# State-space steps of two groups issued as one, with every operation of the stage in a fixed order

## The chip, the cores and the metric

The kernel runs on one core of a Trainium2 chip. The metric is the device time of one execution in microseconds (us). Engine names are those of the profile: PE is TensorE (matmuls; PEld are its weight loads), DVE is VectorE, ACT is ScalarE, POOL is GpSimd, and SP is the queue that issues loads.

## What is computed

One layer of a hybrid block on x of 1024 tokens x 1024 features, in float32. A first projection makes the inputs of two branches: a chunked gMLP (giving `y_a`) and a Mamba-2 state-space mixer (giving `y_b`). The change is in the second branch, which works on 32 heads of width 64 in 8 groups, on 8 chunks of 128 tokens:

```python
y_diag = jnp.einsum('bcgls,bcgrls,bcsgrp->bclgrp', cb, decay, xd)       # inside a chunk
chunk_states = jnp.einsum('bcsgn,bcgrs,bcsgrp->bcgrpn', bc, decay_to_end, xd)
# scan over the chunks: state * chunk_decay + chunk_states, giving prev_states
y_off = jnp.einsum('bclgn,bcgrpn,bcgrl->bclgrp', cc, prev_states, jnp.exp(a_cs))
y_b = y_diag + y_off + xh * d_skip[:, None]
yz = y_b * jax.nn.silu(ssm_z)                   # by groups of 256 features
y_b = rms_norm(yz, ssm_norm_w)                  # one mean square per token and group
merged = sigmoid(g_a) * (y_a @ w_proj_a) + sigmoid(g_b) * (y_b @ w_proj_b)
out = rms_norm(x + gate * (merged @ w_out), final_norm_w)
```

## The kernel before

**Stages.** Normalisation and the projections, the convolution and the gMLP mixing fill the execution up to about 908 us; then comes the stage that the change rewrites, the state-space steps, to about 1114 us; then the product with `w_proj_b` (units p1 to p7, whose first matmul writes the tile `x0p`) and the product with `w_out`. Products are in float32 that is split into a high and a low part, with three matmuls for one.

**A step.** One step is one group g (4 heads) on two chunks; s = 0 to 3 counts the steps of a group, and 32 steps make the stage. `order` (L1295) puts the groups in four rounds of two: (0,0), (1,0), (0,1), (1,1), and so on, so neighbours in `order` are the same s of two groups. Every step has these parts:

- *fetch*: two loads on SP's queue, `dcy` (cumulated decays, broadcast to 128 partitions) and `sl` (x, B, C and the gate of the two chunks).
- *mask* and *decay*: ACT makes `ea` by two exps (L1119), POOL masks `dcy` (L1123), ACT makes `dcy` by eight exps (L1131).
- *prep*: 12 rows of PE fill the banks `pc` (products of C and B, and B transposed) and `px` (x transposed); DVE multiplies `dcy` by `pc` (L1147) and makes `xd` and `xe` from `px` (L1150); ACT copies `bn` from `pc` (L1154).
- *front*: eight PE matmuls 128*64 into `yi` (inside the chunk), then `sp` (state increments; two matmuls 128*128, one where s = 3). DVE adds `sp` to the state that POOL multiplied by the chunk's decay (L1192, L1198 and L1200: chunk 0, then chunk 1, which needs chunk 0's), and adds the skip term to `yi` (L1180, two operations).
- *back*: PE multiplies the two states by C into `yn` (L1211; its second half needs the state after chunk 0), DVE scales it (`ym`, L1226), POOL adds it to `y` (L1228) and multiplies by the gate into `yz` (L1229).

**After every second step of a group** the mean squares follow: `yz` is stored, ACT squares it in place (L1251), POOL sums two tiles (L1255), four PE matmuls 128*32 (`pq`, here *strips*) sum over partitions, DVE makes a row (L1267), the row goes to memory and is read back as a column `ssq`, POOL takes the root by `pow` (L1282), and the root is stored. For the last two groups these are called *late* and fall behind the steps. They write where `yz` is, so they wait for its store.

**Beside the steps** PE works off the product `y_a @ w_proj_a` (`proj_a`, L1463): 8 column blocks of 24 draws, each draw two matmuls 128x512 into the banks `pma`, 384 in all. `draw(n)` puts n draws at its place in PE's order. For a block, ACT makes the high parts `wah` (L1377) and DVE the low parts `wal` (L1382, here *wal*); a gate by DVE closes the block (`tha`, L1488). The operands `yh` (ACT) and `yl` (DVE, L1360) come from `ya_operand(k)`, k = 0 to 7.

**What sets the order.** Each engine runs its instructions in order. `link(key, f)` puts an operation behind the last one linked on that engine; what isn't linked is put in by the scheduler, by its priority. `later(n, f)` runs f n slots of `run_tasks` later, and `beside_step` takes one waiting piece of work (a sum, a root). `load` issues on SP's queue in program order, and `store` on ACT's. Before, a step is: front of step n, decays of n+3, a piece of work, masks of n+4, 8 or 10 `pma`, back of n, prep of n+2.

## Time and profile before

| what | value |
|---|---|
| three runs | 1368.3 us median, 1366.72 to 1368.78 |
| the profiled execution | 1367.94 us, of which the profile's span is 1366.0 |
| clock granted to PE over the span | 0.999 |
| busy: PE, DVE, ACT, POOL | 1352.3, 1045.9, 799.2, 192.5 us |

The profile is one execution. A row of the timeline gives the start, the time to the end of the group and the instruction's form; consecutive instructions of one form stand in one row with their count. Starts are measured, ends of matmuls are modelled, and on every engine records overlap a little; so what an instruction costs its engine is read here from one start to the next. A row of a group gives the count, the busy time, the mean in ns, the idle time ahead of it and what ended that.

### The profile page before, as it was taken

To read this page: it belongs to the slowest core of one execution; us is meant where nothing else is said; L and a number is where in the kernel's file an instruction comes from. 1 tells how busy PE (TensorE), PEld (TensorE's weight loads), DVE (VectorE), ACT (ScalarE), POOL (GpSimd) and SP (SyncE) were. 2 spreads that over 40 slices of the span, in tenths; PEclk is the share of its full clock that TensorE was granted. 3 is DMA by queue.
4 is the path that set the end of the run, shared out by engine and by line. 5 is a ranking of instruction groups with operands and counts; after the bars stand their busy time and mean duration, and the time that the engine had idled before them with its cause. 6 is when DMAs were issued, how large, how long until landed. Compare 5 with 4: busy or idle time off the path is not lost.

```text
span 1366.0 us, 20176 instructions
## 1 busy us (share of the span) xinstructions
PE 1352.3 (99%) x6943; PEld 1116.6 (82%) x6943; DVE 1045.9 (77%) x1716; ACT 799.2 (59%) x1447; POOL 192.5 (14%) x191
## 2 busy tenths in 40 slices
PE   8999999999999999999999999999999999999997
PEld 7688888888888888888888888888888887888886
DVE  4786876777778888697887797458888866859976
ACT  5763666666666656466566556486877834233443
POOL 1000000000000000000000000006798971000002
PEclk9999999999999999999999999999999999999999
DMA  9674444334344657877656675589889959988903
GB/s 286 181 244 135 142 124 120 104 117 124 108 139 139 181 181 230 252 230 241 211 180 189 219 247 167 166 282 314 305 299 307 309 201 320 325 268 322 382 37 124
DMA packets 249530, 288.65 MB, mean 211 GB/s; under 512 B 16812, under 2 KB 196436, under 8 KB 249428
## 3 DMA queue, kind: packets, MB, share of 16 engines
q1 hardware_dynamic: 174868, 203.80, 46.9%
q10 hardware_dynamic: 74560, 83.57, 17.9%
q8 instruction: 55, 0.90, 0.3%
q14 instruction: 47, 0.39, 0.1%
HBM read 199.82 MB, written 87.49 MB: 210 GB/s over the span
## 4 chain that ended last, share of the span: by engine, by line
PE 92%; DMA 3%; DVE 2%; ACT 1%; SPq 1%; issue 0%; POOL 0%; POOLq 0%; DVEq 0%; ACTq 0%
PE xz L565 6%; PE xcb L565 6%; PE xx L565 6%; PE pma L82 6%; PE xuz L565 6%; PE xg L565 6%; PE ox L1867 3%; PE ycb L565 3%; PE vx L954 3%; PE yp L1676 3%; PE yz L565 3%; PE yx L565 3%; PE yg L565 3%; PE yuz L565 3%; PE yi L82 2%; PE sp L82 2%
## 5 line engine op out<-in xcount | busy, mean ns | idle before, releaser
L1123 POOL TENSOR_SCALAR_AFFINE_SELECT dcy<-dcy 128x1024 f32<-128x1024 f32 x32 | 35.3, 1103 | 790.6 <-ACT ea L1119 786.9
L1131 ACT ACTIVATE dcy<-dcy,nacs 128x128 f32<-128x128 f32 x256 | 78.3, 389 | 2.7 <-POOL dcy L1123 2.1
L1147 DVE TENSOR_TENSOR dcy<-dcy,pc 128x1024 f32<-128x1024 f32 x32 | 39.0, 1218 | 8.0 <-PE pc L85 6.4
L1229 POOL TENSOR_TENSOR yz<-y,sl 128x512 f32<-128x512 f32 x32 | 44.4, 1387 | 2.5
L82 PE MATMUL pma<-yh,wah 128*128 128x512 f32 x128 | 43.1, 418 | 0.0
L82 PE MATMUL pma<-yh,wal 128*128 128x512 f32 x128 | 42.5, 413 | 0.0
L82 PE MATMUL pma<-yl,wah 128*128 128x512 f32 x128 | 40.2, 396 | 0.0
L1119 ACT ACTIVATE ea<-dcy 64x512 f32<-64x512 f32 x64 | 39.8, 622 | 0.7 <-DMA dcy<-acs_d 0.3
L1024 ACT ACTIVATE ac<-ac 128x1024 f32<-128x1024 f32 x32 | 33.9, 1061 | 10.2 <-DVE ac L1022 10.0
L1614 DVE SCALAR_TENSOR_TENSOR yn<-yn,par,rb 128x512 f32<-128x512 f32 x32 | 25.4, 793 | 18.6 <-DMA yn<-yb_d 16.9
L1154 ACT COPY bn<-pc 128x256 f32<-128x256 f32 x32 | 11.9, 371 | 46.9 <-DVE dcy L1147 46.9
L1228 POOL TENSOR_TENSOR y<-y,ym 128x512 f32<-128x512 f32 (+1 forms) x32 | 37.0, 1155 | 1.9 <-DVE ym L1226 1.9
L1022 DVE SCALAR_TENSOR_TENSOR ac<-c2x,cwt,ac 128x1023 f32<-128x1023 f32 (+2 forms) x24 | 30.7, 1279 | 6.1 <-ACT ac L1020 6.0
L82 PE MATMUL yi<-dcy,xd 128*64 128x128 f32 x512 | 35.0, 279 | 0.0
L1022 DVE SCALAR_TENSOR_TENSOR ac<-c2cb,cwt,ac 128x1023 f32<-128x1023 f32 (+2 forms) x24 | 30.6, 1274 | 5.6 <-ACT ac L1020 5.5
L1882 POOL TENSOR_TENSOR r<-r,fnw 128x512 f32<-128x512 f32 x4 | 5.3, 1344 | 204.8 <-ACT junk L1880 204.8
L986 ACT ACTIVATE vm<-vm,vr 128x128 f32<-128x128 f32 x64 | 25.8, 484 | 14.2 <-DMA vm<-v_d 13.7
L1226 DVE TENSOR_TENSOR ym<-yn,ea 128x512 f32<-128x512 f32 (+1 forms) x32 | 19.9, 622 | 18.5 <-PE yn L82 18.4
L824 ACT CAST wbb<-wbr 128x512 fp32r<-128x512 f32 x32 | 19.8, 619 | 22.8 <-DMA wb_d<-wbb 17.0
L82 PE MATMUL sp<-xe,bn 128*128 128x256 f32 x112 | 32.7, 409 | 0.0
L82 PEld LDWEIGHTS yn<-sl,st 128*128 128x128 f32 x224 | 29.7, 191 | 2.8 <-POOL st L1192 0.4
L82 PEld LDWEIGHTS yi<-dcy,xd 128*64 128x64 f32 x512 | 27.3, 136 | 5.7 <-issue 3.1
(2963 smaller groups left out, 4372.8 us busy)
## 6 DMA issues: line engine op xcount, KB each, us to landing
sl<-s_d SPq DMA_DIRECT2D x32, 768.0 KB, 6.4
s_d<-ac ACTq DMA_DIRECT2D x32, 512.0 KB, 3.3
wb_d<-wbb ACTq DMA_DIRECT2D x32, 512.0 KB, 3.4
dcy<-acs_d SPq DMA_DIRECT2D x32, 512.0 KB, 5.3
av<-in_w_in_dram SPq DMA_DIRECT2D x36, 256.0 KB, 2.9
aw<-in_ada_w_dram SPq DMA_DIRECT2D x16, 512.0 KB, 6.6
...
```

What stands on the lines that cost most here:

```text
L82: pin(PE.matmul(acc, l, r, start=first, stop=last))
L565: pin(PE.matmul(ps, lw[:, k * P : (k + 1) * P], r[k], start=first and n + k == 0, stop=n == 2 and k == 3, skip_group_check=not first))
L954: pin(PE.matmul(ps[pn][j], l[:, j * P : (j + 1) * P], r, start=nm in ("p1", "p5", "p2") and n + units[i][1] == 0, stop=n == 2 and k == 3, ...
L1022: V.scalar_tensor_tensor(ac[:, s:], cc[:, : S - s], conv_wt[:, 3 - s, i : i + 1], ac[:, s:], op0=ALU.mult, op1=ALU.add)
L1119: link("A", lambda: A.activation(ea[hh * HD : (hh + 1) * HD], dcy.rearrange("p (j e) i l -> p e j (i l)", e=2)[hh * HD : (hh + 1) * HD, hh ...
L1123: link("G", lambda: G.affine_select(out=d8, in_=d8, compare_op=ALU.is_ge, fill=-1e30, base=0, pattern=[[0, 2 * HPG], [1, P]], channel_mult ...
L1131: link("A", lambda: A.activation(dcy[:, h, i, :], dcy[:, h, i, :], AF.Exp, bias=sub[:, i, h : h + 1]))
L1147: link("V", lambda: V.tensor_tensor(d3, d3, pc[:, 0:256].unsqueeze(1).to_broadcast([P, HPG, 256]), op=ALU.mult))
L1228: link("G", lambda: G.tensor_add(y1[:, :, t0:], y1[:, :, t0:], m[:, :, t0:]))
L1229: link("G", lambda: G.tensor_mul(yz, y1, sl[:, 4:6]))
L1676: pin(PE.matmul(ps[j], a[:, v, js], r, start=first and n + k == 0, stop=n == 2 and k == KT - 1, skip_group_check=not first))
L1867: pin(PE.matmul(ps, a[:, tsl], b[:, cs], start=first and n + j == 0, stop=n == 2 and j == 3, skip_group_check=not first))
```

## The change

Steps n and n+1 (one s of both groups of a round) are issued as one, in three parts:

```python
def fronts(n):
    decays(n + 4)
    each(n, "inside")                  # yi of both steps
    ...
        p.strips(q, sq)                # pq of earlier steps
    each(n, "increments")              # sp of both
    each(n, "skip")
    ...
        p.row(q)
    each(n, "add_state", 0)
    second(n)                          # POOL and DVE: the state after chunk 1
    upto("fetch_sums", n + 7)

def backs(n):
    for m in (n, n + 1):
        g, s = order[m]
        groups[g].back(s)              # yn
        if m == n:
            second(n + 1)
        groups[g].close(s)             # ym, y, yz
    if n + 2 < len(order) and order[n + 2][1]:
        each(n + 2, "mul_state", 0)

def preps(n):
    for m in (n, n + 1):
        if m < len(order):
            g, s = order[m]
            groups[g].prep(s)          # pc, px, dcy, xd, bn
            upto("exps", m + 3)
    upto("mask", n + 4)
    each(n, "prep2")                   # xe of both

draw(12)
for n in range(0, len(order), 2):
    item(fronts, n)
    if n == 0:
        for k in (6, 7):
            ya_operand(k)
    ...
        for _ in range(1 if n < 28 else 2):
            beside_step()
    draw(5 if n == 0 else 2)
    item(backs, n)
    ...
    item(preps, n + 2)
    upto("fetch", n + 7)
    run_tasks()
    draw(11 if n == 0 else 7 + n // 2 % 3 % 2)
    run_tasks()
```

A pair of steps here has 4 `pma` between `sp` and `yn`, and 14 or 16 (where n // 2 leaves 1 by 3) behind the preps. The parts below go with it:

```diff
-            A.copy(wh, wr)
+            link("A", lambda: A.copy(wh, wr))
...
-            V.tensor_sub(wl, wr, f32(wh))
+            link("V", lambda: V.tensor_sub(wl, wr, f32(wh)))
...
-                elif k == 3 and dd + 1 < KT:
+                elif k == 5 and dd + 1 < KT:
                     wa_lows(dd + 1)
...
-                store(yb_d[2 * g + j][:, q * 512 : (q + 1) * 512], self.yz[q][:, j])
+                if late:
+                    store(to, yz[:, j])
+                else:
+                    later(5, load, to, yz[:, j])
...
-                pin(A.activation(sq[j], sq[j], AF.Square))
-            G.tensor_add(sq[0], sq[0], sq[1])
+                link("A", lambda: A.activation(self.late[j], self.yz[1][:, j], AF.Square))
...
-            f = lambda: G.tensor_tensor(self.columns(), self.columns(), nhalf, op=ALU.pow)
+                link("V", lambda: V.tensor_scalar(y.bitcast(I32), v.bitcast(I32), -0.5, float(0x5F3759DF),
+                                                  op0=ALU.mult, op1=ALU.add))
+                for _ in range(3):
+                    link("V", lambda: V.tensor_mul(t, y, y))
+                    link("V", lambda: V.scalar_tensor_tensor(t, t, -0.5, v, op0=ALU.mult, op1=ALU.mult))
+                    link("V", lambda: V.scalar_tensor_tensor(y, t, 1.5, y, op0=ALU.add, op1=ALU.mult))
...
-    for k in (6, 7):
-        ya_operand(k)
     masks(3)
     decays(3)
```

So the roots of groups 0 to 5 are ten DVE operations of 128x8 each instead of one on POOL; `wal`, `wah`, the rows, the gates of blocks 0 to 6 and the late squares are linked; the stores of `yz`, of the rows, of the roots and of the gated blocks go on SP's queue; the late squares are written to tiles of their own (`lq`); and the operands of k = 6 and 7 are made behind the first front. The banks of p1's first tiles are taken in another order. PE has the same number of rows before and after.

PE in the middle of the stage. The number behind a name's first underscore is s, the one behind it counts tiles. Before, at a step with s = 1:

```order
L85 MATMUL pc_2_9865<-ident,sl_2_9635 128x128
L85 MATMUL px_2_9864<-ident,sl_2_9635 128x128 x2
L82 MATMUL yi_1_9886<-dcy_1_9554,xd_1_9799 64x128 x8
L82 MATMUL pq_1_9895<-yz_2_9378,ones 32x128 x4
L82 MATMUL sp_1_9902<-xe_1_9801,bn_1_9803 128x256 x2
L82 MATMUL pma_0_9683<-yh_8125,wah_1_9364 128x512
L82 MATMUL pma_1_9686<-yh_8126,wah_1_9364 128x512
L82 MATMUL pma_0_9683<-yl_8127,wah_1_9364 128x512
L82 MATMUL pma_1_9686<-yl_8128,wah_1_9364 128x512
```

And after, at the pair with s = 2 that has its strips in the same place:

```order
L82 MATMUL pma_1_9299<-yh_8028,wal_0_8971 128x512
L82 MATMUL yi_2_9322<-dcy_2_8871,xd_2_9241 64x128 x8
L82 MATMUL yi_2_9331<-dcy_2_9036,xd_2_9259 64x128 x8
L82 MATMUL pq_1_9340<-yz_2_8736,ones 32x128 x4
L82 MATMUL sp_2_9345<-xe_2_9272,bn_2_9243 128x256 x2
L82 MATMUL sp_2_9348<-xe_2_9274,bn_2_9261 128x256 x2
L82 MATMUL pma_0_9296<-yh_8033,wah_0_8970 128x512
L82 MATMUL pma_1_9299<-yh_8034,wah_0_8970 128x512
L82 MATMUL pma_0_9296<-yl_8035,wah_0_8970 128x512
L82 MATMUL pma_1_9299<-yl_8036,wah_0_8970 128x512
L82 MATMUL yn_2_9377<-sl_2_8958,st_8261 128x128 x2
L82 MATMUL yn_2_9377<-sl_2_8958,st 128x128 x2
```

The matmuls 128*64 of two steps and the strips stand together now, where each step had its own block between transposes or `pma` and `sp`; and `yn` follows two draws behind `sp`.

DVE at the start of the stage. Before, `yl` of k = 6 and 7 (tiles 8152 to 8159) stood ahead of the first addition to a state:

```order
L1150 TENSOR_TENSOR xd_0_8248<-px_0_8237,dthq 128x512
L1150 TENSOR_TENSOR xe_0_8250<-px_0_8237,dde 128x512
L1360 TENSOR_TENSOR yl_8152<-yl_8152,yh_8150 128x512
L1360 TENSOR_TENSOR yl_8153<-yl_8153,yh_8151 128x512
L1360 TENSOR_TENSOR yl_8158<-yl_8158,yh_8156 128x512
L1360 TENSOR_TENSOR yl_8159<-yl_8159,yh_8157 128x512
L1198 COPY st<-sp_0_8343 128x256
L1180 SCALAR_TENSOR_TENSOR y_0_8348<-sl_0_7908,dskt,yi_0_8334 128x256 x2
L1382 TENSOR_TENSOR wal_0_8353<-wa_0_8273,wah_0_8352 128x512
L1382 TENSOR_TENSOR wal_1_8356<-wa_1_8275,wah_1_8355 128x512
```

After, they stand behind the preps of steps 2 and 3 (`dcy_1`, `xd_1`, `xe_1`) and the first `wal`:

```order
L1151 TENSOR_TENSOR dcy_1_8263<-dcy_1_8263,pc_1_8428 128x1024
L1155 TENSOR_TENSOR xd_1_8438<-px_1_8427,dthq 128x512
L1151 TENSOR_TENSOR dcy_1_8267<-dcy_1_8267,pc_1_8446 128x1024
L1155 TENSOR_TENSOR xd_1_8456<-px_1_8445,dthq 128x512
L1155 TENSOR_TENSOR xe_1_8469<-px_1_8427,dde 128x512
L1155 TENSOR_TENSOR xe_1_8471<-px_1_8445,dde 128x512
L1423 TENSOR_TENSOR wal_0_8326<-wa_0_8271,wah_0_8325 128x512
L1423 TENSOR_TENSOR wal_1_8329<-wa_1_8273,wah_1_8328 128x512
L1401 TENSOR_TENSOR yl_8152<-yl_8152,yh_8150 128x512
L1401 TENSOR_TENSOR yl_8153<-yl_8153,yh_8151 128x512
L1401 TENSOR_TENSOR yl_8158<-yl_8158,yh_8156 128x512
```

PE's row at that time, after: the first matmul that reads `yl_8152` is in the second draw of k = 6, directly behind the preps of steps 2 and 3:

```order
L85 MATMUL px_1_8445<-ident,sl_1_8269 128x128 x2
L82 MATMUL pma_0_8309<-yh_8131,wal_1_8174 128x512
L82 MATMUL pma_1_8312<-yh_8132,wal_1_8174 128x512
L82 MATMUL pma_0_8309<-yh_8150,wah_1_8173 128x512
L82 MATMUL pma_1_8312<-yh_8151,wah_1_8173 128x512
L82 MATMUL pma_0_8309<-yl_8152,wah_1_8173 128x512
L82 MATMUL pma_1_8312<-yl_8153,wah_1_8173 128x512
```

`yl` of k = 6 has moved behind eight operations of DVE, the third of which, `dcy_1_8267` (step 3), reads what ACT's decay of step 3 makes; PE's matmul that reads it stands straight behind the preps.

DVE at the first root inside the pairs, after (it stands between the preps and the fronts of the pair n = 16):

```order
L1155 TENSOR_TENSOR xe_0_9599<-px_0_9557,dde 128x512
L1155 TENSOR_TENSOR xe_0_9601<-px_0_9575,dde 128x512
L1423 TENSOR_TENSOR wal_0_9459<-wa_0_8878,wah_0_9458 128x512
L1423 TENSOR_TENSOR wal_1_9462<-wa_1_8880,wah_1_9461 128x512
L1314 TENSOR_SCALAR ssq<-ssq 128x8
L1317 TENSOR_TENSOR ssq<-ssq 128x8
L1318 SCALAR_TENSOR_TENSOR ssq<-ssq 128x8
L1319 SCALAR_TENSOR_TENSOR ssq<-ssq 128x8
```

The ten operations of the root (of which four are shown) stand behind `wal` and ahead of the skip terms. On POOL, before, the root stood behind the products of states:

```order
L1228 TENSOR_TENSOR y_2_9341<-y_2_9341,ym_2_9379 128x512
L1229 TENSOR_TENSOR yz_2_9378<-y_2_9341,sl_2_8991 128x2x256
L1192 TENSOR_TENSOR st_8261<-st,cd 128x256
L1192 TENSOR_TENSOR st<-st_8260,cd 128x256
L1282 TENSOR_TENSOR ssq<-ssq,nhalf 128x8
L1123 AFFINE_SELECT dcy_0_9315<-dcy_0_9315 128x1024
L1228 TENSOR_TENSOR y_2_9422<-y_2_9422,ym_2_9459 128x512
L1229 TENSOR_TENSOR yz_2_9458<-y_2_9422,sl_2_9071 128x2x256
```

And after, where POOL has no root, a pair reads so (L1201 are the products of states, L1271 the sum, L1241 and L1242 `y` and `yz`):

```order
L1128 AFFINE_SELECT dcy_3_9038<-dcy_3_9038 128x1024
L1128 AFFINE_SELECT dcy_3_9196<-dcy_3_9196 128x1024
L1201 TENSOR_TENSOR st_8260<-st,cd 128x256
L1271 TENSOR_TENSOR yz_2_8746<-yz_2_8746 128x512
L1201 TENSOR_TENSOR st_8261<-st,cd 128x256
L1241 TENSOR_TENSOR y_2_9351<-y_2_9351,ym_2_9385 128x512
L1242 TENSOR_TENSOR yz_2_9384<-y_2_9351,sl_2_8958 128x2x256
L1241 TENSOR_TENSOR y_2_9354<-y_2_9354,ym_2_9395 128x512
L1242 TENSOR_TENSOR yz_2_9394<-y_2_9354,sl_2_9120 128x2x256
```

The root has left POOL's row, the two masks of a pair stand together, and the sum stands between the products for chunk 1 of the two steps, so that the second step's addition of chunk 1 on DVE, and `ym` behind it, follow the sum.

233 lines of the change are left out of this document (128 added, 105 removed).

## The prediction

> **What bounds the kernel now.** First the page: busy times, and the chain that ended last.
>
> ```profile
> PE 1352.3 (99%) x6943; PEld 1116.6 (82%) x6943; DVE 1045.9 (77%) x1716; ACT 799.2 (59%) x1447; POOL 192.5 (14%) x191
> PE 92%; DMA 3%; DVE 2%; ACT 1%; SPq 1%; issue 0%; POOL 0%; POOLq 0%; DVEq 0%; ACTq 0%
> ```
>
> PE is the bound. The average hides the stage that the change rewrites, so next come the windows (start:end, length, then busy time by PE, PEld, DVE, ACT, POOL, granted clock, DMA share, GB/s) and PE's waits from 905 to 1131 us:
>
> ```profile
> 1050.00:1100.00 50.00, 50.00 (x412) 42.57 (x411) 41.98 (x75) 37.61 (x99) 45.35 (x44) 1.00 0.91 305
> PE pq L82 <- POOL yz L1247: 1.4, 2, 0.8
> ```
>
> In the stage PE never stands still at full clock, with two waits at its end. So a gain can only come from what PE's instructions cost back to back and from those 1.4 us; a loss comes wherever DVE (84% busy here) or POOL (91%) falls behind.
>
> **Gain 1: edges of the 128*64 blocks, 5.6 us.** PE's timeline around one step:
>
> ```profile
> 1001.00 0.38 PE L85 MATMUL px<-ident,sl 128*128 128x128 f32 x2
> 1001.22 0.39 PE L82 MATMUL pc<-sl 128*128 128x128 f32 x2
> 1001.56 0.38 PE L85 MATMUL px<-ident,sl 128*128 128x128 f32 x2
> 1001.87 1.09 PE L82 MATMUL yi<-dcy,xd 128*64 128x128 f32 x16
> 1002.03 0.49 PE L82 MATMUL yi<-dcy,xd 128*64 128x128 f32 x5
> 1002.36 0.61 PE L82 MATMUL yi<-dcy,xd 128*64 128x128 f32 x8
> 1002.89 1.13 PE L82 MATMUL sp<-xe,bn 128*128 128x256 f32 x4
> 1004.32 0.63 PE L82 MATMUL pma<-yl,wah 128*128 128x512 f32 x2
> 1009.28 0.70 PE L82 MATMUL sp<-xe,bn 128*128 128x256 f32 x2
> 1009.63 0.58 PE L82 MATMUL pma<-yh,wal 128*128 128x512 f32 x1
> ```
>
> Two `px` take 0.22 us before `pc`, but 0.31 before `yi`: 0.09. The two halves of a pair of `yi` run beside each other; the first pair takes 0.16 (1001.87 to 1002.03), the next three 0.33, so 0.11 each: 0.05. The last four take 0.53 to `sp` for 0.44: 0.10. Two `sp` more make 0.43 (1002.89 to where the single pair at 1009.28 would put it: 0.78 against 0.35), so four and two `pma` (0.46) should take 1.32 and take 1.43: 0.11. One block's entry and exit cost 0.35 us; `pma` before `yi` costs the same. The changed order has 16 blocks of two steps for 32 of one: 16 x 0.35 = 5.6 us gained, on PE and so in full.
>
> **Gain 2: the late squares, 1.5 us.** Two `pma` as they follow on each other, and the tail before:
>
> ```profile
> 913.52 0.62 PE L82 MATMUL pma<-yh,wal 128*128 128x512 f32 x2
> 913.98 0.62 PE L82 MATMUL pma<-yh,wah 128*128 128x512 f32 x2
> ...
> 1123.18 0.61 PE L82 MATMUL pma<-yh,wah 128*128 128x512 f32 x2
> 1124.37 0.43 PE L82 MATMUL pq<-yz,ones 128*32 128x128 f32 x8 [0.57 <-POOL yz L1247]
> 1128.17 0.42 PE L82 MATMUL pq<-yz,ones 128*32 128x128 f32 x8 [0.84 <-POOL yz L1247]
> 1130.02 0.39 PE L1676 MATMUL x0p<-p1bh,p1a 128*128 128x512 f32 x1
> ```
>
> The squares waited for the store of `yz`. In their own tiles they don't, and by the order 42 `pma` instead of 30 (42 x 0.23 = 9.7 us) stand between the last `yn` and the first late strip. ACT's squares and POOL's sums of two groups are done some 8 us behind that `yn` (two `y` and two `yz` of 1.2 and 1.4, two sums of 1.3), so both waits go: 0.57 + 0.84, with the gaps around them 1.5 from start to start. What is late next is p1's operand, which comes by the row, its store and the root; by the same sums it is ready about 1 us before PE wants it, and I count nothing lost.
>
> **Loss 1: the start, 5.5 us.** ACT, DVE and PE before:
>
> ```profile
> 917.73 0.37 ACT L1154 COPY bn<-pc 128x256 f32<-128x256 f32 x1 [1.65 <-DVE dcy L1147]
> 920.46 2.45 ACT L1131 ACTIVATE dcy<-dcy,nacs 128x128 f32<-128x128 f32 x8 [1.19 <-POOL dcy L1123]
> 925.52 2.45 ACT L1131 ACTIVATE dcy<-dcy,nacs 128x128 f32<-128x128 f32 x8
> 919.42 3.36 DVE L1360 TENSOR_TENSOR yl<-yl,yh 128x512 fp32r<-128x512 f32 x4
> 933.08 1.81 DVE L1382 TENSOR_TENSOR wal<-wa,wah 128x512 fp32r<-128x512 f32 x2
> 912.51 0.70 PE L82 MATMUL pma<-yh,wah 128*128 128x512 f32 x2
> ```
>
> The chain on ACT from 917.73 (`bn`, exps, mask, decay of step 2, `wah`, decay of step 3) is the same in the changed order, so step 3's `dcy` is exponentiated by 927.97. DVE then does `dcy` (1.14), `xd`, two `xe` (0.60 each), two `wal` (0.9 each) and only then `yl` of k = 6 (0.7): 928.0 + 1.1 + 1.8 + 1.8 + 0.7 = 933.4. PE on the same clock: 24 `pma` from 912.51 end at 918.2, two `yi` 1.9 (1.02 as above, and 0.87 without a second set of edges), two `sp` 1.6, ten `pma` 2.5, eight `yn` and twenty transposes and products at 0.11 each 0.9 and 2.1: 927.2, and four `pma` later, at 928.2, it wants `yl`. It waits 5.2 us, and 0.3 for the other half: 5.5. Before, these subtractions ran at 919.42, on a DVE that had nothing else. What hid them was order; nothing queued behind PE's wait can pass it.
>
> **Loss 2: DVE late at the pairs with roots, 4.7 us.** DVE's times from start to start, and the pieces on POOL:
>
> ```profile
> 1026.42 1.20 DVE L1147 TENSOR_TENSOR dcy<-dcy,pc 128x1024 f32<-128x1024 f32 x1
> 1027.54 0.68 DVE L1150 TENSOR_TENSOR xd<-px,dthq 128x512 f32<-128x512 f32 x1
> 1028.14 0.67 DVE L1150 TENSOR_TENSOR xe<-px,dde 128x512 f32<-128x512 f32 x1
> 1028.74 0.27 DVE L1267 TENSOR_SCALAR tri<-pq 128x128 f32<-128x128 f32 x1
> 1028.94 0.41 DVE L1198 COPY st<-sp 128x256 f32<-128x256 f32 x1
> 1029.27 0.85 DVE L1180 SCALAR_TENSOR_TENSOR y<-sl,dskt,yi 128x256 f32<-128x256 f32 x2
> 1030.07 0.42 DVE L1200 TENSOR_TENSOR st<-st,sp 128x256 f32<-128x256 f32 x1
> 151.09 0.16 DVE L111 TENSOR_TENSOR vr<-vr 128x8 f32<-128x8 f32 x1
> 152.50 0.17 DVE L112 SCALAR_TENSOR_TENSOR vr<-vr 128x8 f32<-128x8 f32 x1
> 1023.55 1.28 DVE L1488 SCALAR_TENSOR_TENSOR tha<-tha,pma 128x512 f32<-128x512 f32 x2
> 1023.42 0.62 POOL L1192 TENSOR_TENSOR st<-st,cd 128x256 f32<-128x256 f32 x1
> L1255 POOL TENSOR_TENSOR yz<-yz 128x512 f32<-128x512 f32 x14 | 18.3, 1309 | 0.0
> L1282 POOL TENSOR_TENSOR ssq<-ssq,nhalf 128x8 f32<-128x8 f32 x6 | 9.9, 1653 | 0.0
> ```
>
> The stage never ran on VectorE with a root in it, so its price comes from the nearest row: 128x8 operations that follow on each other, seven steps of 0.20 us from 151.09 to 152.50. Ten are 2.0 us; the bounds are 0 (all in DVE's idle time) and 2.0 on the path. Six roots took 9.9 us from POOL, where they delayed products of states without a wait on PE; that relief is counted at nothing.
>
> Let Y be a pair's first `yi` and A the end of the first addition to a state. From `dcy` to the next A, DVE does two `dcy`, two `xd`, two `xe`, four skips, a row, an addition: 2.3 + 2.4 + 1.6 + 0.2 + 0.3 = 6.8 us, plus extras (`wal` 1.8, `tha` 1.2, root 2.0). `dcy` starts when PE has the first `pc` (Y + 7.85 for s = 1 and 2, 6.96 for s = 0, 6.99 for s = 3) or when DVE is free: A + 4.1 (product, sum and product on POOL, 2.5; an addition; two `ym`), with s = 0 (half of `ym`) 3.6, with s = 3 (no products) 1.5. PE needs A before the second half of `yn`, at Y + 5.45 (s = 0: 5.01; s = 3: 4.59), by 1.9 for two `yi`, 0.4 strips, 1.6 `sp`, 1.1 for four `pma`, 0.4. A pair takes PE 12.31 us (s = 1, 2), 11.42 (s = 0) or 11.45 (s = 3), 0.46 more with 16 `pma`. Pairs are 0 to 15; roots lie ahead of 8, 9, 12 and 13, the other two behind the steps.
>
> - Pair 8 (`wal`, root): 6.99 + 6.8 + 3.8 - 11.91 = 5.68 against 5.01: stall 0.67.
> - Pair 9 (`tha`, root): A + 3.6 = 9.28; + 6.8 + 3.2 - (11.42 + 0.67) = 7.19 against 5.45: 1.74.
> - Pair 11 (`wal`, `tha`) against 4.59: 0.58. Pair 13 (`wal`, root): 7.94 + 6.8 + 3.8 - 11.42 = 7.12 against 5.45: 1.67.
>
> Elsewhere A comes in time. The sum is 4.7; its bounds are 0, if PE's matmuls in fact run ahead of DVE's cover by 2 us less, and 10, if each signal between DVE and POOL in the loop costs 0.2 more.
>
> [...]
>
> Stores on SP's queue, `wah`, `wal` and gates by list, and p1's banks I count at nothing: ACT and the loads keep over 2 us of slack by the order, and loads of `sl`, issued some two pairs ahead (about 24 us), land in 6.4:
>
> ```profile
> sl<-s_d SPq DMA_DIRECT2D x32, 768.0 KB, 6.4
> ```
>
> If that cover goes, rival 3 prices it.
>
> **The sum.** The profiled execution took 1367.94 (span 1366.0 and 1.9 around it), 0.4 under the median of 1368.3. -5.6 - 1.5 + 5.5 + 4.7 = +3.1: 1371.0 by that execution, and on the median 1371.4 us.
>
> **Rivals.**
> 1. DVE keeps pace behind the start: the small operations of a root run in its idle time (8.0 of 50 us in the window above), so that a root costs the loop nothing. By the recurrence above with roots at 0, pair 11 alone stalls, 0.3. It gives 1368.3 - 7.1 + 5.5 + 0.3 = 1367.0, not slower by what can be told. For it speaks that idle time; against it, that the loop's three ends (PE's `pc`, POOL's sum, DVE's list) leave the root no place between `xe` and the skips but in its turn, at 0.20 each. It decides where a root adds under 0.8 to the loop; from there on pairs 9 and 13 stall. [...]
> 2. The other side, faster: no stall at the start. It needs DVE to start step 3's `dcy` by 922.8, so that `yl` is there at 928.2, so step 3's decay made 5.2 us earlier, and DVE in pace as well. Then only the edges and the tail count: 1361.2. Against it stands the chain on ACT from 917.73.
> 3. Stores at the head of SP's queue wait for POOL's `yz` and hold the loads behind them, in order; it costs when such a wait exceeds the lead of a pair (some 12 us), or signals cost more in every loop. Half a us in each of 15 pairs: 1378.
>
> **Chances.** A measurement of this kernel tells 0.2%, 2.7 us: faster is below 1365.6, slower above 1371.0. The forecast has 0.38 (own range 1370 to 1374; 0.05 of it within), rival 1 0.22, rival 2 0.18, rival 3 0.22. So faster 0.18, within 0.27, slower 0.55. The range 1362.0 to 1378.0 leaves out most of rival 2 and a little of rival 3.
>
> **What would show it.** In the changed profile: `yi` blocks of 16 matmuls with one entry and one exit, some 2.0 us; a wait of about 5 us of PE's `pma` for DVE's `yl` near 928; waits of `yn` for DVE's state at pairs 8, 9, 11 and 13 of 0.6 to 1.7 us; ten 128x8 operations in 2.0 us; no wait of the late strips. Without the wait near 928 loss 1 is wrong, and without those of `yn` loss 2; a wait of `yi` for a load would speak for rival 3.

## The result, and the profile after

The changed kernel takes 1412.0 us (median of 5 runs, 1410.2 to 1416.1) against 1368.5 (1366.7 to 1370.2) for the kernel before in the same runs: ratio 1.0317, interval 1.0302 to 1.0331, 43.4 us slower. The prediction said slower, 1371.4 us, range 1362 to 1378. The sign was right; the size was wrong by more than ten times. The profiled execution has a span of 1408.4 us, against 1366.0 before. One execution of e3 below ran at a granted clock of 0.556 and took 2279.4 us; it is not counted.

The page's busy line, and the window in which PE had been busy for 50.00 of 50 us at clock 1.00 (columns as in the prediction):

```profile
PE 1359.5 (97%) x6943; PEld 1119.9 (80%) x6943; DVE 1066.6 (76%) x1776; ACT 800.1 (57%) x1447; POOL 180.2 (13%) x185
```

```profile
1050.00:1100.00 50.00, 43.38 (x358) 35.88 (x356) 39.78 (x82) 31.70 (x83) 34.41 (x34) 1.00 0.79 264
```

For the same 6943 instructions PE is busy 7.2 us longer than before (1359.5 against 1352.3) and stands still 35.2 us longer (48.9 against 13.7). In the window it stands still for 6.6 of the 50 us, and no other engine is fuller than before: DVE, ACT and POOL fell from 41.98, 37.61 and 45.35 us to 39.78, 31.70 and 34.41. So no engine became the bound by its work. The engines wait for each other in a ring. PE's waits from 900 to 1180 us (what waited, for what, us in total, times, longest), the eight largest of thirteen lines that make 36.0 us, where there had been 1.4:

```profile
PE pma L82 <- DVE yl L1401: 6.5, 1, 6.5
PE x0p L1759 <- ACT p1a L1739: 5.6, 1, 5.6
PE pc L82 <- DVE st L1210: 4.0, 2, 2.7
PE sp L82 <- ACT bn L1161: 3.6, 2, 3.2
PE yn L82 <- DVE y L1192: 3.5, 1, 3.5
PE yi L82 <- DVE xe L1155: 3.3, 3, 1.3
PE sp L82 <- ACT dcy L1136: 3.1, 2, 1.9
PE yn L82 <- DVE st L1210: 1.9, 3, 0.9
```

The prediction had expected two of these eight, the first and the last (the last stands at pairs 9, 11 and 15). The spans divide by place as follows; a pair is counted from the start of its first `yi` to that of the next pair, and the stage ends at the first `x0p` (1130.0 before, 1168.9 after). The number of `pma` in a stretch differs between the two kernels, their sum doesn't; one costs 0.23 us:

| stretch | before | after | difference | `pma` more | difference at equal `pma` |
|---|---|---|---|---|---|
| up to the first `yi` | 915.4 | 918.5 | +3.1 | 12 | +0.3 |
| pair 0 (the start) | 18.5 | 23.8 | +5.3 | -16 | +9.0 |
| pairs 1 to 4 | 49.1 | 47.9 | -1.2 | 0 | -1.2 |
| pairs 5 to 14 | 123.0 | 150.2 | +27.2 | 6 | +25.8 |
| pair 15 to `x0p` | 24.1 | 28.5 | +4.4 | -2 | +4.9 |
| behind `x0p` | 236.0 | 239.6 | +3.6 | 0 | +3.6 |

The first line is work that has changed places: 24 `pma` stand ahead of the first `yi` where 12 stood.

**The start.** PE's rows at the wait for `yl`:

```profile
936.44 1.40 PE L82 MATMUL pma<-yl,wah 128*128 128x512 f32 x2 [6.53 <-DVE yl L1401]
937.63 1.05 PE L82 MATMUL pma<-yh,wal 128*128 128x512 f32 x2
938.49 1.05 PE L82 MATMUL pma<-yh,wah 128*128 128x512 f32 x2
939.34 0.71 PE L82 MATMUL pma<-yl,wah 128*128 128x512 f32 x2
```

The wait is the one forecast, 6.53 us in place of 5.2. What was not forecast stands behind it: two `pma` take 0.86 us (937.63 to 938.49) where the prediction's rows have 0.46, until about 939.5. The granted clock in that stretch, and the same at the end, behind the wait of 5.6 us for `p1a`:

```profile
936.00:940.00 4.00, 3.56 (x9) 2.69 (x10) 2.18 (x4) 3.16 (x11) 0.00 (x0) 0.56 0.89 278
1168.00:1175.00 7.00, 6.13 (x14) 4.37 (x14) 6.85 (x12) 4.65 (x9) 0.00 (x0) 0.52 1.05 378
```

These two waits of PE are paid a second time in clock: 0.56 and 0.52 of full speed in the stretches behind them. At the start the clock is at half until 939.53, so that the slow matmuls last from 936.4 for 3.1 us; behind the wait for `p1a` and in two other kernels the slow work was longer, 5.7 to 6.3 us (last section). Four stretches of half clock in the change (932.70, 1024.86, 1041.93 and 1168.22, with 3.09, 3.00, 3.41 and 6.18 us) hold 15.7 us of PE's work, half of which is about the 7.2 us by which it is busy longer.

**The pairs.** Three mechanisms are visible in the rows. One is the queue. `yz` is squared in its own tile by ACT, so ACT waits until the stores of `yz` have read it. Those stores now stand on SP's queue, five slots later and behind loads. SP's and ACT's rows:

```profile
1011.48 4.15 SPq L91 DMA_DIRECT2D yb_d<-yz  x4
```

```profile
1020.84 2.56 ACT L1267 ACTIVATE yz<-yz 128x512 f32<-128x512 f32 x4 [6.01 <-DMA yb_d<-yz]
```

The second is the ring of the `yz` tiles. It has four tiles, and the second group's sum, hence its strips on PE, come one pair later than the first group's. By the kernel's ring, POOL's last `yz` of a pair wants the tile that those strips, in the next pair's front, still have to read; the profile names no releaser ("issue"). POOL's row, and PE's a little ahead of it:

```profile
1112.40 1.27 POOL L1242 TENSOR_TENSOR yz<-y,sl 128x512 f32<-128x512 f32 x1 [4.95 <-issue]
```

```profile
1111.81 0.43 PE L82 MATMUL pq<-yz,ones 128*32 128x128 f32 x8
```

POOL stands 4.95 us and goes on 0.6 us after the strips have begun, and where the strips come a pair earlier (e2), the wait is gone. In the stage the two make 28.4 us of POOL and 25.8 of ACT, in six waits each (the view of waits, 935 to 1170 us):

```profile
POOL yz L1242 <- issue: 28.4, 6, 5.6
ACT yz L1267 <- DMA yb_d<-yz: 25.8, 6, 6.0
```

The third is the root on DVE. DVE's rows of one root, and POOL's rows beside it:

```profile
1112.22 0.17 DVE L1317 TENSOR_TENSOR ssq<-ssq 128x8 f32<-128x8 f32 x1
1112.42 1.27 DVE L1318 SCALAR_TENSOR_TENSOR ssq<-ssq 128x8 f32<-128x8 f32 x1
1113.72 0.54 DVE L1319 SCALAR_TENSOR_TENSOR ssq<-ssq 128x8 f32<-128x8 f32 x1
1114.29 0.54 DVE L1317 TENSOR_TENSOR ssq<-ssq 128x8 f32<-128x8 f32 x1
1114.86 1.00 DVE L1318 SCALAR_TENSOR_TENSOR ssq<-ssq 128x8 f32<-128x8 f32 x1
1115.90 1.01 DVE L1319 SCALAR_TENSOR_TENSOR ssq<-ssq 128x8 f32<-128x8 f32 x1
```

```profile
1113.62 1.18 POOL L1201 TENSOR_TENSOR st<-st,cd 128x256 f32<-128x256 f32 x2
1114.76 2.13 POOL L1128 TENSOR_SCALAR_AFFINE_SELECT dcy<-dcy 128x1024 f32<-128x1024 f32 x2
```

An operation of 0.17 us takes 1.27 when POOL's `yz` of 1.27 starts with it (1112.40 and 1112.42), 0.54 beside POOL's products of 0.57 each, 1.00 beside its masks of 1.07 each. In these rows the small operation lasts as long as POOL's; where POOL had nothing to do (the root at 1038.73), all ten took 0.16 or 0.17. What ties the two engines is not shown. This root took 5.5 us, not 2.0; the four roots in the pairs took 2.0, 3.4, 3.4 and 5.5.

**What went as forecast.** PE's rows of one pair's `yi`, and of the two late strips:

```profile
1052.09 1.97 PE L82 MATMUL yi<-dcy,xd 128*64 128x128 f32 x32
...
1158.40 0.42 PE L82 MATMUL pq<-lq,ones 128*32 128x128 f32 x8
...
1161.26 0.43 PE L82 MATMUL pq<-lq,ones 128*32 128x128 f32 x8
```

The block has one entry and one exit, and the late strips wait no more. But p1's first product waits in their stead:

```profile
1168.87 0.79 PE L1759 MATMUL x0p<-p1bh,p1a 128*128 128x512 f32 x1 [5.59 <-ACT p1a L1739]
```

### The profile page after: what moved, and what is told of

It is laid out like the page before. It is cut to its first block, busy times and chain, and to the rows that moved or that the text cites. A ratio compares the mean times of both kernels' runs of the same rounds, so it can differ in the third digit from the quotient of the medians.

```text
span 1408.4 us, 20251 instructions
## 1 busy us (share of the span) xinstructions
PE 1359.5 (97%) x6943; PEld 1119.9 (80%) x6943; DVE 1066.6 (76%) x1776; ACT 800.1 (57%) x1447; POOL 180.2 (13%) x185
## 3 DMA queue, kind: packets, MB, share of 16 engines
q1 hardware_dynamic: 181892, 214.86, 47.9%
q10 hardware_dynamic: 67536, 72.51, 15.3%
## 5 line engine op out<-in xcount | busy, mean ns | idle before, releaser
L1136 ACT ACTIVATE dcy<-dcy,nacs 128x128 f32<-128x128 f32 x256 | 76.8, 388 | 25.9 <-POOL dcy L1128 25.8
L1242 POOL TENSOR_TENSOR yz<-y,sl 128x512 f32<-128x512 f32 x32 | 41.5, 1296 | 30.5 <-issue 28.4
L1192 DVE SCALAR_TENSOR_TENSOR y<-sl,dskt,yi 128x256 f32<-128x256 f32 x64 | 27.1, 474 | 16.2 <-POOL yz L1242 7.8
L1241 POOL TENSOR_TENSOR y<-y,ym 128x512 f32<-128x512 f32 (+1 forms) x32 | 37.2, 1163 | 14.6 <-DVE ym L1239 13.7
L1697 DVE SCALAR_TENSOR_TENSOR yn<-yn,par,rb 128x512 f32<-128x512 f32 x32 | 23.8, 747 | 19.9 <-DMA yn<-yb_d 19.9
L1210 DVE TENSOR_TENSOR st<-st,sp 128x256 f32<-128x256 f32 x48 | 19.1, 416 | 25.9 <-POOL st L1201 20.5
L82 PE MATMUL yi<-dcy,xd 128*64 128x128 f32 x512 | 31.7, 276 | 4.1 <-DVE xe L1155 3.3
L82 PEld LDWEIGHTS pma<-yl,wah 128*128 128x128 f32 x128 | 24.5, 196 | 12.3 <-DVE yl L1401 7.2
L82 PE MATMUL yn<-sl,st 128*128 128x128 f32 x224 | 28.7, 278 | 5.4 <-DVE y L1192 3.5
```

Source lines behind the costliest of these rows:

```text
L82: pin(PE.matmul(acc, l, r, start=first, stop=last))
L1136: link("A", lambda: A.activation(dcy[:, h, i, :], dcy[:, h, i, :], AF.Exp, bias=sub[:, i, h : h + 1]))
L1192: link("V", lambda: V.scalar_tensor_tensor(y1[:, j], sl[:, 2 + j], dskt[:, 2 * g + j : 2 * g + j + 1], self.yi[:, j * 256 : (j + 1) * 256] ...
L1241: link("G", lambda: G.tensor_add(y1[:, :, t0:], y1[:, :, t0:], m[:, :, t0:]))
L1242: link("G", lambda: G.tensor_mul(yz, y1, sl[:, 4:6]))
```

## The experiments

Each edit is made to the changed kernel unless another is named, and no kernel leaves out any of the work. "Above" is (ratio - 1) x 1368.5 us; where an edit stands in an earlier run, its diff isn't repeated.

| run | edits | median us | ratio to before, interval | above, us |
|---|---|---|---|---|
| the change | | 1412.0 | 1.0317 (1.0302 to 1.0331) | 43.4 |
| e1 | start | 1404.2 | 1.0250 (1.0233 to 1.0267) | 34.2 |
| e2 | sums | 1422.0 | 1.0383 (1.0367 to 1.0398) | 52.4 |
| e3 | stores | 1406.9 | 1.0269 (1.0252 to 1.0286) | 36.8 |
| e4 | start, sums, stores, roots' stores | 1403.4 | 1.0250 (1.0232 to 1.0268) | 34.2 |
| e5 | start, all stores, roots by POOL | 1392.9 | 1.0169 (1.0150 to 1.0188) | 23.1 |
| e6 | as e5, and sums | 1388.1 | 1.0135 (1.0114 to 1.0155) | 18.5 |
| e7 | roots by POOL | 1414.4 | 1.0324 (1.0303 to 1.0345) | 44.3 |
| e8 | roots' and blocks' stores | 1412.7 | 1.0318 (1.0297 to 1.0340) | 43.5 |
| e9 | `xe` | 1416.1 | 1.0341 (1.0322 to 1.0359) | 46.7 |
| e10 | sums, and roots staggered | 1416.7 | 1.0340 (1.0320 to 1.0361) | 46.5 |
| e11 | as e6, and `xe`, early roots | 1376.6 | 1.0054 (1.0035 to 1.0073) | 7.4 |
| e12 | second sum behind | 1419.8 | 1.0366 (1.0348 to 1.0384) | 50.1 |
| e13 | as e6, and `xe` | 1377.6 | 1.0056 (1.0036 to 1.0077) | 7.7 |
| e14 | as e6, and early roots | 1388.2 | 1.0138 (1.0121 to 1.0155) | 18.9 |
| e15 | as e11, second sum behind | 1384.7 | 1.0109 (1.0088 to 1.0130) | 14.9 |
| e16 | before, late squares in own tiles | 1369.5 | 1.0001 (0.9992 to 1.0010) | 0.1 |
| e17 | as e15, strips later | 1378.1 | 1.0057 (1.0045 to 1.0070) | 7.8 |
| e18 | as e13, roots by DVE again | 1388.1 | 1.0137 (1.0118 to 1.0157) | 18.7 |

### One edit at a time: start, sums, stores

Start, e1: the last two operands `yl` ahead of the loop again.

```
     pairs_done.append("")
+    for k in (6, 7):
+        ya_operand(k)
     masks(3)
...
-        if n == 0:
-            for k in (6, 7):
-                ya_operand(k)
```

> The changed kernel with the operands of k = 6 and 7 made where they were before, ahead of the steps. My theory: the wait of 6.5 us of pma for yl near 930 goes, and with it about 1.7 us in which matmuls behind that wait run at half pace, so some 8 us less than the changed kernel: 1402 to 1406, and no wait of pma for yl. Rival (the later waits of PE only move up, since DVE, POOL and ACT are what is late): under 3 us less, above 1409.

Measured: 9.2 us of the 43.4 (43.4 - 34.2). PE's row at the place has no wait for `yl`, and two `pma` take 0.62 again:

```profile
929.26 0.62 PE L82 MATMUL pma<-yl,wah 128*128 128x512 f32 x2
```

Pair 0 takes 16.2 us, not 23.8. The wait of 6.5 us and the half clock (3.1 us for work of some 1.5) are about these 7.6: loss 1 by the prediction's mechanism, with the clock behind it on top. The rest of the 9.2 isn't assigned. In this run's profile pairs 5 to 14 take 154.2 us, 4.0 more than in the change's, so something of the rival may be in it.

Sums, e2: both groups' sums of squares in one pair.

```
-            for _ in range(1 if n < 28 else 2):
+            for _ in range(2):
                 beside_step()
```

> The changed kernel with two pieces of work taken at each pair, so that both groups' sums, and so both strips, stand one pair earlier than the second group's did. My theory: POOL's yz of the second group waits six times (28.4 us) for strips that stand in PE's next front, because its tile of four in the ring is still to be read; here that wait is gone, and PE gains 10 to 18 us: 1394 to 1402. Rival (DVE's list with roots is what is late): under 4 us less, above 1408, the same waits for DVE.

The expectation fell: 9 us slower. In the profiles, whose spans differ by 11.4 us, 5.1 more stand between the first `yi` and `x0p` (the stage, in what follows), and 7.1 more behind `x0p` (the table at e8 below). POOL's six waits for the strips did go (the view of waits has no such line any more), but both strips, rows and therefore roots of two groups now fall in one pair. DVE's first and last row of the two roots, of 20 rows, and PE's row there:

```profile
1039.69 0.16 DVE L1314 TENSOR_SCALAR ssq<-ssq 128x8 int32<-128x8 int32 x1
...
1043.37 0.17 DVE L1319 SCALAR_TENSOR_TENSOR ssq<-ssq 128x8 f32<-128x8 f32 x1
1043.48 1.66 DVE L1192 SCALAR_TENSOR_TENSOR y<-sl,dskt,yi 128x256 f32<-128x256 f32 x4
```

```profile
1044.50 3.75 PE L82 MATMUL sp<-xe,bn 128*128 128x256 f32 x8 [4.66 <-DVE y L1192]
```

Even with no operation longer than 0.17 us, two roots hold DVE for 3.8 us, and the skip terms `y` stand behind them in its list. PE waits 4.66 us until `y` has read its bank, and runs eight `sp` in 3.75 us where 1.99 is their usual time.

Stores, e3: the stores of `yz` on ACT's queue at once, as before.

```
-                if late:
-                    store(to, yz[:, j])
-                else:
-                    later(5, load, to, yz[:, j])
+                store(to, yz[:, j])
```

> The changed kernel with the stores of yz on ACT's queue at once, as before, not later on SP's. My theory: ACT's squares wait six times (25.8 us) for the store to land, because it stands behind loads on SP's queue; here these waits are under 1 us each, and PE gains 6 to 14 us: 1398 to 1406. Rival (the squares have slack, and ACT's wait costs PE nothing): under 3 us less, above 1409.

6.6 us by the ratios; the median lies just above the range. ACT's waits for these stores fell from 25.8 to 2.9 us (the same view):

```profile
ACT yz L1264 <- DMA yb_d<-yz: 2.9, 4, 1.2
```

23 us of waiting taken from ACT brought PE 6.6. POOL's waits for the strips stayed (25.8 us in six); that most of ACT's waiting had stood beside them is argued, not shown.

### Several at once, and roots on POOL

The stores of the roots alone (in e4), and those of the rows and of the tanh blocks besides (in e5 and e6), go back to ACT's queue:

```
-            (load if self.g < NG - 2 else store)(rs_d[self.g].rearrange("o (p c) -> (o p) c", p=P),
+            store(rs_d[self.g].rearrange("o (p c) -> (o p) c", p=P),
...
-                later(2, load, to, row[0:P:32, :])
+                nc.scalar.dma_start(to, row[0:P:32, :])
...
-                    later(2, load, mt_d[dd][:, h * 512 : (h + 1) * 512], ths[h])
+                    nc.scalar.dma_start(mt_d[dd][:, h * 512 : (h + 1) * 512], ths[h])
```

e4: start, sums, stores and the roots' stores.

> The changed kernel with the three edits together, and the stores of the roots on ACT's queue, so that they no longer stand ahead of p1's loads on SP's. My theory: what is left of the change is the gain at the edges (5.6 us) and the late squares (1.5), less what DVE is late at the pairs with roots (up to 5): 1361 to 1368. Rival (roots and DVE's list are most of the 43 us): above 1385.

It fell: 34.2 us remained, no less than with the start alone. In the profiles the stage is 11.6 us shorter than e1's, but what stands behind `x0p` is 6.7 us longer. PE's longest waits in the pairs were again those for `y` behind two roots:

```profile
PE sp L82 <- DVE y L1192: 9.3, 2, 5.2
```

e5 leaves out the sums, takes all the stores and gives the roots back to POOL:

```
-                v, n = self.columns(), NG * NCH
...
-                    link("V", lambda: V.scalar_tensor_tensor(y, t, 1.5, y, op0=ALU.add, op1=ALU.mult))
+                self.roots = self.columns()
+                link("G", lambda: G.tensor_tensor(self.roots, self.roots, nhalf, op=ALU.pow))
```

> The changed kernel with the start, all stores' queues (ACT) and the roots (POOL) as before: what stays is the issue of two steps as one by lists, one sum per pair, and the late squares in own tiles. If the second group's strips, one pair behind POOL's yz that needs their tile, are a cause, POOL waits six times for about 5 us, and it takes 1375 to 1390. Rival (queues, roots and start were all of it): 1361 to 1368.

20.3 us came back, and the time, 1392.9, lies just above the range. e6 is e5 with both sums in one pair:

> The same with two sums per pair, so that both strips stand ahead of the yz that needs their tiles. With the strips a cause: 1361 to 1367, 10 to 20 us under the run with one sum, since with roots on POOL nothing of DVE is doubled by it. Rival (the strips' place costs PE nothing): within 3 us of the run with one sum.

4.6 us came, where 10 to 20 were expected. But in the profiles the stage did become 13.5 us shorter (221.7 against 235.2), and what stands behind `x0p` became 6.5 us longer; e6's profiled execution is also the fastest of its four. POOL's waits for the strips are gone here too. PE's are now for `xe` (3.4 us in two), for `p1a` (2.8) and, behind `x0p`, for the bank that `tha` reads (4.4). e7 is the change with only the roots given back to POOL:

> The changed kernel with the roots of groups 0 to 5 on POOL by pow, nothing else undone. My theory: the ten small operations of a root took 2.0 to 5.4 us of DVE at pairs 8, 9, 12 and 13 and stood in the way of PE; 4 to 10 us less than the changed kernel: 1402 to 1408. Rival (DVE waits for POOL at these pairs anyway): within 3 us of 1412, or above it, since POOL has 1.65 us more at six places.

Nothing (44.3 against 43.4). PE's wait for `y` is gone, but those of `pc` for `st` grew from 4.0 us in two to 6.5 in four, and pairs 8, 9 and 13 are even later (16.9, 17.0 and 21.4 us). That three or four causes add up had to be given up with these runs: where one wait is taken away, another stands close behind it.

### Tail, banks, and the order of roots

e8 is the change with the stores of the roots and of the tanh blocks on ACT's queue; those of the rows stay on SP's.

> The change, but the stores of the rows (row sums), of the roots and of the tanh blocks go on ScalarE's queue at once, as before the change; all else as in the change. Theory, SyncE's queue in the tail: the loads of p1's operands stood on SyncE's queue behind the stores of the roots and blocks, which waited for their values; PE waited 5.6 us for p1a and then ran some 3.5 us at half the clock. Without them on that queue the wait falls under 2 us: 1402 to 1406 us. Rival, the roots: p1's factors wait for the roots of groups 4 and 5 whichever queue they go by; the wait stays over 4 us: 1408 to 1412.

It fell: nothing was gained. The rival's mechanism did not hold either. With these stores on ACT's queue the first load of `yn` for p1 is issued at 1154.34, not 1161.77, and the wait of `x0p` falls from 5.6 to 2.6 us, not over 4. (In the change the half clock behind that wait held 6.18 us of PE's work, 1168.22 to 1175.05, not 3.5.) But the next product waits in its place, for DVE's `tha`. It reads nothing of `tha`; by the kernel's banks, what ties the two is the bank of `pma`, which `tha` empties (PE's waits, 1140 to 1180, and one of e6):

```profile
PE x1p L1759 <- DVE tha L1529: 5.9, 1, 5.9
PE x0p L1759 <- ACT p1a L1739: 2.6, 1, 2.6
...
PE x3p L1748 <- DVE tha L1519: 4.4, 1, 4.4
```

This wait bears on more runs than e8. The last `tha` runs 6 to 8 us behind the first `x0p` in every profile. In some kernels a product of p1 wants its bank before that, in the others none does, and edits that touch neither `tha` nor p1 (the sums, `xe`) turned it on and off. What decides it is not shown. By the profiles, in us:

| kernel | first `yi` to `x0p` | behind `x0p` | wait for `tha`'s bank |
|---|---|---|---|
| before | 214.6 | 236.0 | none |
| the change | 250.4 | 239.6 | none |
| e1 | 247.5 | 239.0 | none |
| e2 | 255.5 | 246.7 | 6.3 |
| e4 | 235.9 | 245.7 | 3.8 |
| e5 | 235.2 | 238.4 | none |
| e6 | 221.7 | 244.9 | 4.4 |
| e8 | 248.4 | 245.1 | 5.9 |
| e9 | 248.0 | 245.9 | 4.0 |
| e10 | 250.5 | 247.3 | 6.3 |
| e12 | 254.2 | 245.9 | 7.3 |
| e13 | 218.7 | 240.5 | none |
| e14 | 223.9 | 244.6 | 4.0 |
| e18 | 230.4 | 237.5 | none |

The other profiles have no such wait, and 237.7 to 240.7 us behind `x0p`. So two kernels on different sides of this wait differ by some 4 to 10 us that are not the edit's work in the stage.

`xe`, e9: the second scaled copy directly behind the first, so that the bank of the transposed x is free sooner.

```
-            xd = scaled("xd", dthq)
+            xd, xe = scaled("xd", dthq), scaled("xe", dde)
...
-        each(n, "prep2")
```

> The change, but the second scaled copy xe stands directly behind xd in VectorE's list again, so that the bank of the transposed x is released one pair of operations sooner. Theory, bank held too long: PE's waits for xe at the start of yi and pma (3.3 us and some 1 us in the stretch 900:1180) go and nothing takes their place: 1407 to 1410 us. Rival, VectorE is short by its whole work and only the place of the wait moves: the waits for st, y or bn grow by what those for xe fall: 1411 to 1414.

Nothing, or a loss of 3 us, above both ranges. The waits of `yi` for `xe` fell from 3.3 to 0.8 us, those for `y` grew from 3.5 to 4.4, those for `st` did not grow. In the profiles the stage became 2.4 us shorter; what took the gain away is the wait for `tha`'s bank, with 6.3 us more behind `x0p`. So neither the theory nor the rival held. Staggered, e10: sums as in e2, and `later(5 + 5 * (self.g % 2), self.root)`.

> The change with both groups' sums in one pair (as in the run with the sums alone) and, besides, the root of every odd group one pair of steps later, so that no pair holds two roots. [...] Rival: the pairs with a root are late whatever their number, since GpSimd now runs its sums beside the root at once: 1410 to 1420.

One root in each pair was to bring 1396 to 1406 us. It fell as well, by that range: 46.5 us above, 6 better than both roots in one pair, still not better than the change. In the profiles its stage is as long as the change's, and the loss stands behind `x0p`.

Early roots, e11 and e14: `later(3 ...)` in place of `later(5 ...)` for the row's load and the root of groups 4 and 5.

> The kernel of the run with the start, the stores on ScalarE's queue, the roots by GpSimd's pow and both sums in one pair (1388 us), with xe directly behind xd besides, and the rows' load and root of groups 4 and 5 two slots sooner each. Theory: what was left there were waits for the bank (3.1 us, xe), for p1a (2.8), for tanh behind it (4.4) and the half clock behind each; the first goes by xe's place, the second by the earlier roots: 1378 to 1384 us. Rival: the waits for p1's operands and tanh are one chain of ScalarE's own work, which neither edit touches, and xe's place pushes the state's addition back by as much: 1386 to 1389.

36 of the 43.4 us were back, more than expected. Of the three waits named, the one for `xe` (e6, 3.07 us until 1033.29) had no half clock behind it: 1.00 from 1000 to 1050 us. Two runs share it out:

> The kernel of 1388 us (start, stores on ScalarE's queue, roots by GpSimd's pow, both sums in one pair) with xe directly behind xd alone. It shares out the 11.5 us that this and the earlier roots of groups 4 and 5 won together. Theory, bank of x: the wait of 3.1 us and the one of 1.2 us for xe go: 1381 to 1385. Rival: all came from the tail: 1387 to 1390.

> The kernel of 1388 us with the rows' load and the roots of groups 4 and 5 two slots sooner each, alone. Theory, tail: the waits for p1a and tanh (2.8 and 4.4 us) fall, and the half clock behind them with them: 1379 to 1384. Rival: the bank of x was the whole gain: 1387 to 1390.

The run with `xe` alone has all of it (18.5 to 7.7 us), the early roots have none. The same edit that was worth nothing on the change itself brings 10.8 us here. By the profiles most of this difference is not the bank of the transposed x. `xe` shortens the stage by 3.0 us here (221.7 to 218.7) and by 2.4 on the change; but here it comes with the end of the wait for `tha`'s bank (4.4 us less behind `x0p`), and there with its beginning. The rest of the 10.8 the two profiles don't show.

### The place of the second sum on POOL

In e11 both sums, 2.5 us of POOL, stand ahead of the second group's state. e12 puts the second sum behind the pair's last products in the change itself; e15 does it in e11, with the roots two slots later besides.

```
-            for _ in range(1 if n < 28 else 2):
-                beside_step()
+            beside_step()
         draw(5 if n == 0 else 2)
         item(backs, n)
+        with tc.high_priority():
+            beside_step()
```

> The change with one edit: the first group's sum of squares stays where it is, the second group's stands in the same pair behind the pair's last products (y, yz) on GpSimd, not one pair later. Theory, place of the sum on GpSimd: the sums alone (1422 us) removed the six waits of GpSimd for the strips and lost it again because both sums, 2.5 us, stood ahead of the second group's state on GpSimd; with only one ahead of it, as in the change, the six waits go and nothing is paid: 1398 to 1406 us. Rival: the pair is late for other work whatever stands on GpSimd (VectorE with the roots beside it): 1409 to 1420.

> The kernel of 1376.6 us (both edits), with the second group's sum behind the pair's last products on GpSimd and the roots of groups 0 to 3 two slots later, behind the states. Theory, place of the sum: the waits of 2.2 us for st and 1.7 for ym, which stood behind two sums ahead of the second group's state, go, with what lies behind them: 1366 to 1372, about the kernel before. Rival: VectorE and GpSimd pass the same work on and the wait comes back at the next bank: 1375 to 1379.

Both fell, and e15's time lies outside its rival's range too. In e12 both groups' roots are in one pair again, as in e2, and PE's waits for `y` are the longest in the pairs (10.3 us in two). In e15 the waits for `st` and `ym` shrink, but the sum is now late for the strips:

```profile
PE pq L82 <- POOL yz L1264: 7.5, 3, 5.4
```

e17 gives the strips 2 us more, by putting them behind the increments on PE, and leaves the last pairs as in e11.

> The kernel of 1376.6 us with the second group's sum behind the pair's last products (as in the run that came to 1384.7), the strips behind the increments on TensorE (2 us later than there) and both sums of the last pairs ahead again, as in the kernel of 1376.6. Theory: the sum's place costs on one side the state (2.2 us, 1.7) when it is ahead, on the other the strips (1.5, 1.4, 1.1 and 5.5 us) when it is behind; strips behind the increments leave room for both: 1367 to 1372. Rival: the sum that is late for the strips is late for the next instructions too, and the wait only moves to the bank behind: 1374 to 1380.

7.8 us above, the same as e11 (7.4) and e13 (7.7): the rival held. The sum's place passes a wait on and does not pay for it.

### Two terms of the prediction by themselves

Late squares, e16: the kernel before, in which only the last squares get tiles of their own.

```
-            sq = self.late
+            yz, self.late = self.late, [turn(r, f"lq{self.g}{j}", F32) for j, r in enumerate((ym_r, y1_r))]
+            sq = self.late
             for j in range(2):
-                pin(A.activation(sq[j], sq[j], AF.Square))
+                pin(A.activation(sq[j], yz[j], AF.Square))
```

> The kernel before with one part of the change: the last squares of groups 6 and 7 go to tiles of their own instead of over the products that are still being stored. It measures the second gain of the prediction by itself (1.5 us: the tail's strips waited for those squares). Theory: 1366 to 1368, a gain of 1 to 2 us. Rival: p1's first operand waits for the roots whenever the strips run, so nothing moves: within 0.5 us.

Nothing: 1.0001, interval 0.9992 to 1.0010, which excludes the 1.5 us forecast (0.9989). One of the two waits of the late strips went, the other stayed:

```profile
1127.98 0.42 PE L82 MATMUL pq<-lq,ones 128*32 128x128 f32 x8 [0.67 <-POOL lq L1248]
```

Roots, e18: e13's kernel with the roots by DVE again.

> The kernel of 1377.5 us (start, stores on ScalarE's queue, both sums in one pair, xe behind xd, roots by GpSimd's pow) with the roots by VectorE again, as in the change. It measures the prediction's second loss (4.7 us) by itself where the other waits are gone. Theory, VectorE held beside GpSimd: a root takes 3.4 to 5.5 us in place of 2.0 and two stand in one pair: 8 to 14 us slower, 1386 to 1392. Rival, the price of the prediction (2.0 us each, some hidden): 1379 to 1383. Third: the roots alone in the change's own setting were worth nothing (1414.4 without them), so nothing here either: 1376 to 1379.

11.0 us by the ratios (18.7 - 7.7), inside the theory's range; the prediction had 4.7, with 10 as its upper bound. Pair 8 takes 22.0 us in place of 15.3 and pair 12 17.5 in place of 11.9. First and last of the 20 rows on DVE between 1022.86 and 1027.6 and the skip terms behind them; then PE's row of eight `sp`, and the granted clock behind the wait:

```profile
1022.86 1.05 DVE L1307 TENSOR_SCALAR ssq<-ssq 128x8 int32<-128x8 int32 x1
...
1027.45 0.17 DVE L1312 SCALAR_TENSOR_TENSOR ssq<-ssq 128x8 f32<-128x8 f32 x1
1027.54 1.66 DVE L1188 SCALAR_TENSOR_TENSOR y<-sl,dskt,yi 128x256 f32<-128x256 f32 x4
```

```profile
1028.56 3.75 PE L82 MATMUL sp<-xe,bn 128*128 128x256 f32 x8 [6.03 <-DVE y L1188]
```

```profile
1028.00:1034.00 6.00, 5.45 (x13) 4.39 (x14) 3.19 (x10) 1.40 (x3) 1.23 (x2) 0.50 0.29 107
```

4.7 us of DVE, all of it ahead of `y`, became 6.7 us of the pair: 4.7, and about 1.8 by which eight `sp` at a clock of 0.50 last longer than their 1.99. The theory's mechanism is the smaller part: of the 20 operations only the first, 1.05 us, lasted longer than 0.17. The four roots in the pairs took 2.9, 2.0, 3.5 and 2.0 us; what costs is that two stand in one pair ahead of `y`, and the clock behind the wait. In the change itself no pair holds two.

## Why the prediction was right in sign and wrong in size

**Gain 1, edges, held.** The 32 `yi` stand as one block. Pairs 2 and 14 hold the same matmuls in both kernels and have no wait: they take 11.95 and 12.30 us where they took 12.30 and 12.65, 0.35 each, as forecast. In the other pairs waits, or `pma` and strips that changed places, cover it, so the 5.6 us of all 16 are not shown.

**Gain 2, late squares, failed.** Its step was that p1's operand "is ready about 1 us before PE wants it, and I count nothing lost". In the change the strips stopped waiting and p1's operand then came 5.6 us late; with the squares alone (e16) nothing moved that could be told: in the profile the last pair is 0.8 us shorter, and what stands behind `x0p` 1.7 longer. In the change that operand is late because the roots of groups 4 and 5, on DVE beside POOL, were done at 1157.4 and 1160.4, and the loads for p1 stood on SP's queue behind the roots' stores. Moving these stores (e8) moved the wait, not the end.

**Loss 1, the start, right in mechanism, too small.** 5.5 us forecast, 9.2 measured (e1), 7.6 of it in pair 0: the wait was 6.5, and the half clock behind it was missing from the sum.

**Loss 2, the pairs, failed in both of its steps.** The first is the price of a root, "Ten are 2.0 us". It came from a place where POOL stood idle (nothing of it from 147.8 to 160 us); two of the four roots in the pairs took 3.4 us and one 5.5, beside POOL. In one clean kernel the roots cost 11.0 us (e18), though there two stood in a pair and the clock added to it. The second is "PE needs A before the second half of `yn`", as if that were the only place of a pair where PE waits for DVE. PE also needs the bank that `y`, `xe` or `st` still reads, from `yi` and `sp` to the first `yn`; that is where the 6.03, the 4.66 and the 3.5 us stand. Pairs 8, 9, 11 and 13, forecast 0.7, 1.7, 0.6 and 1.7 late, take 15.7, 15.3, 13.5 and 18.2 us where they took 11.8, 12.6, 11.8 and 12.6. Pairs 5 to 7, which the prediction left free, lost 9.1 us together.

**"Stores on SP's queue ... I count at nothing" failed.** The reason given was the slack of the loads. The loads did not suffer; the reader of the stored tile did. ACT squares `yz` in place, and a late store holds it: 6.6 us (e3). Nothing in the prediction followed a tile to its next writer. The ring of four `yz` tiles and the banks belong to the same omission, and by the stage the ring is the largest single item: in kernels without the other waits the sums shortened it by 13.5 us (e6 against e5) and `xe` by 3.0 (e13 against e6). By the whole time these were 4.6 and 10.8, because the wait for `tha`'s bank came with e6 and went with e13.

**Rival 3** had the queue and a time of 1378, but by another mechanism, loads held behind stores. No wait of PE for a load stands in the pairs; behind them it is what held p1's loads by 7.4 us (e8), without gain when it was removed. Rivals 1 and 2 had nothing for them.

The gains add up only in one order. By that order they are: start 9.2 (e1), stores and roots with them 11.1 more (e5 against e1), sums 4.6, `xe` 10.8: 35.7 of 43.4. The order of the middle terms is a choice, since the singles (6.6 for the stores, -0.9 for the roots, -9.0 for the sums, -3.3 for `xe`) don't add to this; and the last two terms, like the singles of the sums and of `xe`, hold the wait for `tha`'s bank on one side only. The last 7.7 us stay open in part. The profile of e13 (span 1377.0, 11.0 above the profile before) has 4.5 of its 11.0 behind `x0p`, where p1 starts late and at half clock, and waits of 0.8 to 1.8 us for `ym`, `xe`, `y` and `st` in pairs 5, 8 and 13; e15 and e17 show that moving the sum does not remove them. Profiled spans lie between 3 us above and 5 us below the medians, so this division is good to a few us. No version found is faster than the kernel before.
